# First doubling of the triangular inverses: sixteen 128x128 problems against one compact tile on the array's four diagonal 32x32 corners

## The chip, the cores and the metric

One core of one Trainium2 chip. The metric is the device time of one execution in microseconds, median of the runs of the same kernel on the same chip. The names used below: TensorE (PE, its weight load is PEld), VectorE (DVE), ScalarE (ACT), GpSimd (POOL) and SyncE (SP), which issues the DMAs.

## What is computed

One residual block with 512 tokens and 1024 features in float32: a SwiGLU FFN, a token mixer, a second FFN. The mixer has two groups of heads, a multi-head latent attention and a gated delta rule. The change touches the delta rule alone, which solves for every head (4) and every chunk of 64 tokens (8 of them) a unit lower triangular system:

```python
decay = jnp.exp(jnp.where(incl, G[..., :, None] - G[..., None, :], -jnp.inf))
kk = jnp.einsum('bhncd,bhnsd->bhncs', k, k)
A = jnp.where(strict, beta[..., :, None] * kk * decay, 0.0)
M = A + jnp.eye(CHUNK, dtype=A.dtype)
rhs = jnp.concatenate([v * beta[..., None], k * (beta * jnp.exp(G))[..., None]], axis=-1)
W = lax.linalg.triangular_solve(M, rhs, left_side=True, lower=True, unit_diagonal=True)
u, wk = W[..., :GDN_DV], W[..., GDN_DV:]
```

The kernel works with blocks of 128 tokens in place of 64 (the recurrence allows any chunk), so it needs sixteen inverses of 128x128: four blocks p times four heads h.

## The kernel before, in words

The kernel runs FFN 1, the mixer and FFN 2 one after the other; nearly all of TensorE's work is dense products with weights, each made of three products of rounded halves (lines 475 to 477 and 360). Within the mixer the small work is written as Python generators. A step of such a generator emits a few instructions and yields. `dense_units` (line 1469) emits two k-tiles of a weight product, that is six matmuls of 512 columns, and then steps the sides: `chain` (delta rule), `deltas` (its other operands) and `att` (attention). The framework then orders each engine's instructions by its own estimate of when they are ready, except where the code ties one instruction behind another (`follow`, line 149); so the order on TensorE is near to the order of emission, not equal to it.

The chain of the delta rule is: `delta_k`, `delta_a` (the matrix A of every head, transposed, as tile `at`, one per head, with the four blocks p side by side), then `bases()` (line 2264), then `solving` (products with the inverses, lines 1923 and 1932) and the recurrence over the blocks (`recur`, lines 1958 to 1985).

`bases()` builds the sixteen inverses by doubling. `base_blocks` inverts the 16x16 diagonal blocks row by row on VectorE and brings them through DRAM into the tile `t16`: 128 rows, and per problem q = 4p + h 16 columns. Then `inverse(p)` makes, for one block p, the inverses of the 32x32 diagonal blocks of all four heads: it spreads `t16` into a block-diagonal tile `t` of 128 x (4 heads x 128) with the mask `dmask` (line 1808), turns each 32x32 square of it (`flip`, line 1804) into `u`, multiplies with A (line 1814), masks the product with `lmask` into `Y` (line 1816), multiplies again (line 1820), subtracts (line 1822) and turns the result (line 1804 again). The four generators `inverse(0)` to `inverse(3)` stand in one `Side` of width 4 and are stepped in turn: three steps each, twelve in all, of which the last of each emits nothing. `inverse_levels` does the next two doublings, 32 to 64 (lines 1852 to 1868) and 64 to 128 (lines 1880 to 1901); the first of them already uses 32x32 matmuls at two places of the array, rows 0 and columns 32, rows 64 and columns 96, and packs its results 32 columns per problem.

The masks are made once, during FFN 1 (`masks`, line 1367), on GpSimd.

Of the kernel before, what the change touches and what calls it, by code (L numbers as in the profile page):

```python
# [16 lines left out]
ALU = mybir.AluOpType  # L17
AX = mybir.AxisListType

P = 128  # L20
# [3 lines left out]
NB = NT // P  # L24
# [75 lines left out]
class Block:  # L100
# [1266 lines left out]
    def masks(self):  # L1367
        nc = self.nc
        tile = self.slot(s="mk")
        room = iter([tile[:, i * P:(i + 1) * P] for i in range(4)])  # L1370
        g = nc.gpsimd
        half = next(room).bitcast(BF16)
        self.eye, self.emask = half[:, :P], half[:, P:]
        nc.vector.tensor_copy(self.eye, self.ident)
        g.memset(self.emask, 0.0)
        g.affine_select(out=self.emask, in_=self.emask, pattern=[[1, P]], compare_op=ALU.is_ge, fill=-1.0e30, base=0,
                        channel_multiplier=-1)
        self.triu = next(room)
        g.affine_select(out=self.triu, in_=self.ones, pattern=[[1, P]], compare_op=ALU.is_ge, fill=0.0, base=0,
                        channel_multiplier=-1)  # L1380
        self.dmask = next(room)
        dv = self.dmask.rearrange("p (j i) -> p j i", i=16)
        g.affine_select(out=dv, in_=self.ones.rearrange("p (j i) -> p j i", i=16), pattern=[[-16, 8], [0, 16]],
                        compare_op=ALU.is_ge, fill=0.0, base=0, channel_multiplier=1)
        g.affine_select(out=dv, in_=dv, pattern=[[16, 8], [0, 16]], compare_op=ALU.is_ge, fill=0.0, base=15,
                        channel_multiplier=-1)
        self.lmask = next(room)
        mv = self.lmask.rearrange("p (j i) -> p j i", i=16)
        g.affine_select(out=mv, in_=self.ones.rearrange("p (j i) -> p j i", i=16), pattern=[[-16, 8], [0, 16]],
                        compare_op=ALU.is_ge, fill=0.0, base=-16, channel_multiplier=1)  # L1390
        g.affine_select(out=mv, in_=mv, pattern=[[16, 8], [0, 16]], compare_op=ALU.is_ge, fill=0.0, base=31,
                        channel_multiplier=-1)
        g.memset(mv[:, 1:8:2, :], 0.0)

        am = self.const([P, 192], BF16, s="am")
        g.memset(am, 0.0)
        g.memset(am[0:1, 0:64], 1.0)
        g.memset(am[0:1, 128:192], -1.0e30)
        self.amask = am[:, :P], am[:, P:]
        sel = self.slot(F32R, s="sel")  # L1400
        g.memset(sel.bitcast(F32), 0.0)
        self.sel = sel.rearrange("p (h c) -> p h c", h=4)
        for o in (0, 32):
            nc.vector.tensor_copy(self.sel[o:o + 4], self.ident[o:o + 4, o:o + 4].unsqueeze(2).to_broadcast([4, 4, P]))
# [386 lines left out]
        yield  # L1791
        yield

    def inverse(self, p):

        nc = self.nc
        h4 = lambda x: x.rearrange("p (h d) -> p h d", h=4)
        hs = lambda h: slice(h * P, (h + 1) * P)
        at = lambda h, rows=slice(0, P), c0=0, c1=P: self.at[h][rows, p * P + c0:p * P + c1]

        def flip(src):

            t = self.slot(s="T")
            nc.vector.transpose(out=t, in_=src)
            return t

        t = self.slot(s="t0")
        self.mul(t.rearrange("p (h i c) -> p h i c", h=4, i=8),
                 self.t16[:, 4 * p:4 * p + 4, :].unsqueeze(2).to_broadcast([P, 4, 8, 16]),
                 self.dmask.rearrange("p (i c) -> p i c", i=8).unsqueeze(1).to_broadcast([P, 4, 8, 16]))  # L1810
        u = flip(t)
        py = self.aux()
        for h in range(4):
            nc.tensor.matmul(py[:, hs(h)], at(h), t[:, hs(h)], start=True, stop=True)
        y = self.slot(s="Y")
        self.mul(h4(y), h4(py), self.lmask.unsqueeze(1).to_broadcast([P, 4, P]))
        yield
        pz = self.aux()
        for h in range(4):
            nc.tensor.matmul(pz[:, hs(h)], y[:, hs(h)], u[:, hs(h)], start=True, stop=True)  # L1820
        un = self.slot(s="U")
        nc.vector.tensor_tensor(out=un, in0=u, in1=pz, op=ALU.subtract)
        t = flip(un)
        yield

        self.un[p], self.tn[p] = un, t

    def inverse_levels(self):

        nc = self.nc  # L1830
        h4 = lambda x: x.rearrange("p (h d) -> p h d", h=4)
        at = lambda p, h, rows, c0, c1: self.at[h][rows, p * P + c0:p * P + c1]
        un, each = self.un, [(p, h) for p in reversed(range(NB)) for h in range(4)]
        sides = [(j, slice(j, j + 32), slice(j + 32, j + 64)) for j in (0, 64)]

        @contextmanager
        def together():
            with self.traced() as block:
                yield
            after = None  # L1840
            for i in block:
                if i.engine == mybir.EngineType.PE:
                    if after:
                        self.follow(i, after)
                    after = i.name

        py, y = self.aux(), self.slot(s="Y")
        with together():
            for p, h in each:
                c = P * p + 32 * h  # L1850
                for j, a, b in sides:
                    nc.tensor.matmul(py[b, c:c + 32], at(p, h, a, j + 32, j + 64),
                                     self.tn[p][a, h * P + j:h * P + j + 32], start=True, stop=True,
                                     tile_position=(j, j + 32))
        nc.scalar.copy(y[sides[0][2], :], py[sides[0][2], :])
        nc.vector.tensor_copy(y[sides[1][2], :], py[sides[1][2], :])
        yield
        yield
        pz = self.aux()
        with together():  # L1860
            for p, h in each:
                c = P * p + 32 * h
                for j, a, b in sides:
                    nc.tensor.matmul(pz[a, c:c + 32], y[b, c:c + 32], un[p][b, h * P + j + 32:h * P + j + 64],
                                     start=True, stop=True, tile_position=(j + 32, j))
        for p in reversed(range(NB)):
            for j, a, b in sides:
                nc.vector.tensor_scalar(out=h4(un[p][a, :])[:, :, j + 32:j + 64],
                                        in0=pz[a, P * p:P * p + P].rearrange("p (h c) -> p h c", h=4), scalar1=-1.0,
# [3 lines left out]
        a, b = slice(0, 64), slice(64, P)  # L1873
# [1 line left out]
        at64 = lambda p, h: slice(256 * (p % 2) + 64 * h, 256 * (p % 2) + 64 * h + 64)  # L1875
        pts, ts, ys = [self.aux() for _ in pairs], [self.slot(s="T") for _ in pairs], [self.slot(s="Y") for _ in pairs]
        both = [(n, p, h) for n, ps in enumerate(pairs) for p in reversed(ps) for h in range(4)]
        with together():
            for n, p, h in both:
                nc.tensor.transpose(pts[n][a, at64(p, h)], un[p][a, h * P:h * P + 64], self.ident[a, a])  # L1880
        for t, pt in zip(ts, pts):
# [1 line left out]
        yield  # L1883
        yield
        pys = [self.aux() for _ in pairs]
        with together():
            for n, p, h in both:
                nc.tensor.matmul(pys[n][b, at64(p, h)], at(p, h, a, 64, P), ts[n][a, at64(p, h)], start=True, stop=True,
                                 tile_position=(0, 64))
# [2 lines left out]
        yield  # L1892
        yield
        pzs = [self.aux() for _ in pairs]
        with together():
            for n, p, h in both:
                nc.tensor.matmul(pzs[n][a, at64(p, h)], ys[n][b, at64(p, h)], un[p][b, h * P + 64:h * P + P], start=True,
                                 stop=True, tile_position=(64, 0))
        for n, ps in reversed(list(enumerate(pairs))):
            for p in ps:  # L1900
                nc.vector.tensor_scalar(out=h4(un[p][a, :])[:, :, 64:],
                                        in0=pzs[n][a, 256 * (p % 2):256 * (p % 2) + 256].rearrange("p (h c) -> p h c", h=4),
# [314 lines left out]
    def mixer(self, norms):  # L2217
        nc, tc = self.nc, self.tc
# [19 lines left out]
            for t in tiles:  # L2238
                self.table(t, t, AF.Silu, after=after)

        self.inv, self.un, self.tn = ([None] * NB for _ in range(3))
        self.kd, self.us, self.o, self.wk, self.vb, self.kbg = ([None] * NB for _ in range(6))
        self.S = None

# [18 lines left out]

        def bases():
            yield from self.base_blocks()
            inv = Side(wide=4)
            inv.add(*(self.inverse(p) for p in range(NB)))
            while inv.open or inv.todo:
                inv.step()
                yield  # L2270
            yield from self.inverse_levels()

        chain.add(self.delta_k(kT), self.delta_a(kT), bases())
        self.dense_units(4, Rates(sides, (1, 0, 1.5)), 1, conv_done(0, qT))
        silu(qT)
# [23 lines left out]
        fill = Side()  # L2299
# [203 lines left out]
```

## Time and profile before

| | before |
|---|---|
| median of 3 runs | 1021.51 us (1021.45 to 1022.29) |
| profiled execution, own time | 1021.74 us |
| its span | 1020.0 us |
| outside the span | 1.74 us |
| TensorE busy | 1010.3 us (99%) |
| VectorE busy | 809.1 us (79%) |
| ScalarE busy | 513.5 us (50%) |
| GpSimd busy | 28.9 us (3%) |

How to read it: the span is the time from the first to the last instruction of one execution. Matmuls are pipelined, so a busy time of TensorE adds records that overlap; what a batch of matmuls costs on the path is read from the chain of waits, which gives every piece the time from the end of the piece before it to its own end. A float32 matmul (as opposed to the rounded halves) stands in the trace as two records, each with a weight load of its own. A row "x8" is eight such records merged.

### The profile page before, as it was taken

How to read it: one execution, taken by the hardware profiler on the slowest of the kernel's cores; microseconds unless marked ns; L12 is line 12 of the kernel's file. 1: busy time of each engine (PE TensorE's matmuls, PEld its weight loads, DVE VectorE, ACT ScalarE, POOL GpSimd, SP SyncE). 2: the span in 40 equal slices, each digit the busy share in tenths (PEclk: the TensorE clock that was granted, in tenths of full speed). 3: DMA queues.
4: the chain of work that ended last, by engine and by line, in shares of the span. 5: the costliest groups of instructions: out<-in, count | busy, mean ns of one | idle time of the engine just before them, and what ended most of it. 6: DMA issues, size and time to landing. Idle time of an engine off the chain costs nothing.

```text
span 1020.0 us, 17205 instructions
## 1 busy us (share of the span) xinstructions
PE 1010.3 (99%) x6729; PEld 908.1 (89%) x6729; DVE 809.1 (79%) x1428; ACT 513.5 (50%) x921; POOL 28.9 (3%) x74
## 2 busy tenths in 40 slices
PE   7999999999999999999999999999999999999998
PEld 6788899999887899888888888998999999987988
DVE  4789788887787847878988658777888888789995
ACT  4453455556422225558846465464555555634443
POOL 0000000000200000100000011000000000000000
PEclk9999999999999999999999999999999999999999
DMA  9998233333688835321222210213233333372612
GB/s 326 291 280 263 63 104 108 100 115 110 187 295 292 284 74 173 82 62 42 67 73 52 70 36 21 84 49 96 85 102 106 107 102 110 113 253 72 175 42 63
DMA packets 203775, 130.79 MB, mean 128 GB/s; under 512 B 14241, under 2 KB 188334, under 8 KB 203694
## 3 DMA queue, kind: packets, MB, share of 16 engines
q1 hardware_dynamic: 203694, 129.70, 42.1%
q8 instruction: 53, 0.87, 0.3%
q14 instruction: 28, 0.23, 0.1%
HBM read 127.18 MB, written 2.49 MB: 127 GB/s over the span
## 4 chain that ended last, share of the span: by engine, by line
PE 95%; DVE 3%; DMA 1%; issue 0%; ACT 0%; SPq 0%; POOL 0%; DVEq 0%
PE pa L360 17%; PE pa L475 16%; PE pa L476 15%; PE pa L477 15%; PE pb L360 13%; PE pa L1228 3%; PE pb L1228 2%; PE pb L2186 1%; PE pb L2166 1%; PE pb L475 1%; PE pb L476 1%; PE pb L477 1%; PE pb L1735 1%; PE pb L673 1%; DMA vecs<-in_b_ada 1%; DVE cv L1679 1%
## 5 line engine op out<-in xcount | busy, mean ns | idle before, releaser
L275 DVE TENSOR_TENSOR wl<-wr,wh 128x1024 fp32r<-128x1024 f32 x105 | 128.2, 1222 | 45.1 <-ACT wh L279 45.0
L234 ACT CAST wh<-wr 128x1024 fp32r<-128x1024 f32 (+1 forms) x87 | 87.3, 1012 | 146.5 <-PE pa L476 121.3
L475 PE MATMUL pa<-hh,wh 128*128 128x512 f32 (+1 forms) x357 | 137.2, 384 | 0.0
L477 PE MATMUL pa<-hh,wl 128*128 128x512 f32 (+1 forms) x357 | 134.9, 378 | 0.0
L476 PE MATMUL pa<-hl,wh 128*128 128x512 f32 (+1 forms) x357 | 134.7, 377 | 0.0
L235 DVE TENSOR_TENSOR wl<-wr,wh 128x1024 fp32r<-128x1024 f32 (+1 forms) x87 | 101.5, 1172 | 41.3 <-ACT wh L234 41.1
L279 ACT CAST wh<-wr 128x1024 fp32r<-128x1024 f32 x105 | 107.4, 1052 | 13.0 <-DVE wr L275 7.2
L475 PE MATMUL pa<-ah,wh 128*128 128x512 f32 (+1 forms) x294 | 110.5, 376 | 0.0
L476 PE MATMUL pa<-al,wh 128*128 128x512 f32 (+1 forms) x294 | 110.1, 374 | 0.0
L477 PE MATMUL pa<-ah,wl 128*128 128x512 f32 (+1 forms) x294 | 109.7, 373 | 0.0
L475 PEld LDWEIGHTS pa<-hh,wh 128*128 128x128 f32 x357 | 67.3, 189 | 13.1 <-issue 1.6
L844 DVE SCALAR_TENSOR_TENSOR aa<-ar,sc,aa 128x512 f32<-128x512 f32 x98 | 73.5, 750 | 6.8 <-DMA ar<-in_w_ada 4.9
L477 PEld LDWEIGHTS pa<-hh,wl 128*128 128x128 f32 x357 | 67.2, 188 | 12.0
L476 PEld LDWEIGHTS pa<-hl,wh 128*128 128x128 f32 x357 | 67.3, 189 | 10.7
L275 DVE TENSOR_TENSOR wr<-wr,wr 128x512 f32<-128x512 f32 x105 | 72.5, 690 | 2.0
L360 PE MATMUL pa<-hh,wh 128*128 128x256 f32 x240 | 68.0, 283 | 0.0
L360 PE MATMUL pa<-th,wh 128*128 128x256 f32 x240 | 67.9, 283 | 0.0
L360 PE MATMUL pa<-tl,wh 128*128 128x256 f32 x240 | 67.9, 283 | 0.0
L360 PE MATMUL pa<-th,wl 128*128 128x256 f32 x240 | 67.9, 283 | 0.0
L360 PE MATMUL pa<-hl,wh 128*128 128x256 f32 x240 | 67.9, 283 | 0.0
L360 PE MATMUL pa<-hh,wl 128*128 128x256 f32 x240 | 67.9, 283 | 0.0
L475 PEld LDWEIGHTS pa<-ah,wh 128*128 128x128 f32 x294 | 55.3, 188 | 12.2 <-ACT wh L234 2.5
(485 smaller groups left out, 2619.1 us busy)
## 6 DMA issues: line engine op xcount, KB each, us to landing
wr<-in_ffn_w_in SPq DMA_DIRECT2D x79, 512.0 KB
ar<-in_w_ada SPq DMA_DIRECT2D x96, 256.0 KB
wr<-in_ffn_w_out SPq DMA_DIRECT2D x32, 512.0 KB
ar<-in_w_ada SPq DMA_DIRECT2D x22, 512.0 KB
wr<-in_w_in SPq DMA_DIRECT2D x21, 512.0 KB
wr<-in_ffn_w_out SPq DMA_DIRECT2D x16, 384.0 KB
wr<-in_w_out SPq DMA_DIRECT2D x8, 512.0 KB
wr<-in_ffn_w_in SPq DMA_DIRECT2D x8, 384.0 KB
```

The source lines that it names most:

```text
L234: self.nc.scalar.copy(hi, raw)
L235: self.nc.vector.tensor_tensor(out=lo, in0=raw, in1=hi.bitcast(F32), op=ALU.subtract)
L275: sub = lambda out, x, y: nc.vector.tensor_tensor(out=out, in0=x, in1=y, op=ALU.subtract)
L279: nc.scalar.copy(hi[:, :n], raw[:, :n])
L360: nc.tensor.matmul(z, a[:, j, :], b, start=start and j == 0 and i == 0, stop=j == 3 and i == 2, skip_group_check=not start)
L475: mm(out, wh, xh, start=start, stop=False)
L476: mm(out, wh, xl, start=False, stop=False)
L477: mm(out, wl, xh, start=False, stop=stop)
L673: nc.tensor.matmul(pg[32 * q:32 * q + 32, :256], self.sc[:, kc:kc + 1].to_broadcast([P, 32]), a[kc], start=(e == 0), stop=(e == 1), tile_p ...
L844: nc.vector.scalar_tensor_tensor(out=acc, in0=a, scalar=sc, in1=acc, op0=ALU.mult, op1=ALU.add)
L1228: nc.tensor.matmul(z, a[:, j, :], b, start=start and j == 0 and i == 0, stop=j == 3 and i == 2, skip_group_check=not start)
L1679: nc.vector.scalar_tensor_tensor(out=a[:, d:], in0=p[:, :NT - d], scalar=wj(3 - d), in1=a[:, d:], op0=ALU.mult, op1=ALU.add)
```

## The change

The first doubling is done once, for all sixteen problems, in one tile of 128 x (16 problems x 32 columns) in place of four tiles of 128 x (4 heads x 128). For each problem q and each diagonal 32x32 block j there is one 32x32 matmul at `tile_position=(32j, 32j)`, that is 64 matmuls in each of the two products, tied in order by `together` (now a method). The mask of `t16` has two columns (`halves`), `lmask` 32. The 32x32 inverses stay packed as `u32` and `t32`, which `inverse_levels` reads directly; four VectorE or GpSimd multiplications with `quads` spread `u32` into the four block-diagonal tiles `un[p]`. `inverse` is one generator with five yields.

```diff
         self.triu = next(room)
...
-        self.dmask = next(room)
...
+        room = next(room)
+        by16, self.halves, self.quads, self.lmask = room[:, :8], room[:, 8:10], room[:, 12:16], room[:, 32:64]
+        g.affine_select(out=by16, in_=self.ones[:, :8], pattern=[[-16, 8]], compare_op=ALU.is_ge, fill=0.0, base=0,
+                        channel_multiplier=1)
+        g.affine_select(out=by16, in_=by16, pattern=[[16, 8]], compare_op=ALU.is_ge, fill=0.0, base=15,
                         channel_multiplier=-1)
...
+        nc.vector.tensor_reduce(out=self.halves, in_=by16.rearrange("p (j e) -> p e j", e=2), axis=AX.X, op=ALU.add)
+        nc.vector.tensor_reduce(out=self.quads, in_=by16.rearrange("p (j e) -> p j e", e=2), axis=AX.X, op=ALU.add)
+        g.memset(self.lmask[:, 16:], 0.0)
+        nc.vector.tensor_copy(self.lmask[:, :16], self.halves[:, 1:2].to_broadcast([P, 16]))
...
-    def inverse(self, p):
+    def inverse(self):
...
+        q32 = lambda x: x.rearrange("p (q c) -> p q c", q=16)
+        spots = [(q, j, slice(32 * j, 32 * j + 32), slice(32 * q, 32 * q + 32)) for q in reversed(range(16))
+                 for j in range(4)]
...
         t = self.slot(s="t0")
-        self.mul(t.rearrange("p (h i c) -> p h i c", h=4, i=8),
-                 self.t16[:, 4 * p:4 * p + 4, :].unsqueeze(2).to_broadcast([P, 4, 8, 16]),
-                 self.dmask.rearrange("p (i c) -> p i c", i=8).unsqueeze(1).to_broadcast([P, 4, 8, 16]))
+        self.mul(t.rearrange("p (q e c) -> p q e c", q=16, e=2),
+                 self.t16.unsqueeze(2).to_broadcast([P, 16, 2, 16]),
+                 self.halves.unsqueeze(1).unsqueeze(3).to_broadcast([P, 16, 2, 16]))
         u = flip(t)
+        yield
         py = self.aux()
-        for h in range(4):
-            nc.tensor.matmul(py[:, hs(h)], at(h), t[:, hs(h)], start=True, stop=True)
+        with self.together():
+            for q, j, rows, cols in spots:
+                c = P * (q // 4) + 32 * j
+                nc.tensor.matmul(py[rows, cols], self.at[q % 4][rows, c:c + 32], t[rows, cols], start=True, stop=True,
+                                 tile_position=(32 * j, 32 * j))
         y = self.slot(s="Y")
-        self.mul(h4(y), h4(py), self.lmask.unsqueeze(1).to_broadcast([P, 4, P]))
+        self.mul(q32(y), q32(py), self.lmask.unsqueeze(1).to_broadcast([P, 16, 32]))
+        yield
         yield
         pz = self.aux()
-        for h in range(4):
-            nc.tensor.matmul(pz[:, hs(h)], y[:, hs(h)], u[:, hs(h)], start=True, stop=True)
-        un = self.slot(s="U")
-        nc.vector.tensor_tensor(out=un, in0=u, in1=pz, op=ALU.subtract)
-        t = flip(un)
-        yield
-
-        self.un[p], self.tn[p] = un, t
+        with self.together():
+            for q, j, rows, cols in spots:
+                nc.tensor.matmul(pz[rows, cols], y[rows, cols], u[rows, cols], start=True, stop=True,
+                                 tile_position=(32 * j, 32 * j))
+        self.u32 = self.slot(s="U")
+        nc.vector.tensor_tensor(out=self.u32, in0=u, in1=pz, op=ALU.subtract)
+        self.t32 = flip(self.u32)
+        yield
+        for p in reversed(range(NB)):
+            self.un[p] = self.slot(s="U")
+            self.mul(self.un[p].rearrange("p (h j c) -> p h j c", h=4, j=4),
+                     q32(self.u32)[:, 4 * p:4 * p + 4].unsqueeze(2).to_broadcast([P, 4, 4, 32]),
+                     self.quads.unsqueeze(1).unsqueeze(3).to_broadcast([P, 4, 4, 32]), nc.gpsimd if p % 2 else None)
+        yield
...
-                                     self.tn[p][a, h * P + j:h * P + j + 32], start=True, stop=True,
+                                     self.t32[a, c:c + 32], start=True, stop=True,
...
-                    nc.tensor.matmul(pz[a, c:c + 32], y[b, c:c + 32], un[p][b, h * P + j + 32:h * P + j + 64],
+                    nc.tensor.matmul(pz[a, c:c + 32], y[b, c:c + 32], self.u32[b, c:c + 32],
...
         def bases():
             yield from self.base_blocks()
-            inv = Side(wide=4)
-            inv.add(*(self.inverse(p) for p in range(NB)))
-            while inv.open or inv.todo:
-                inv.step()
-                yield
+            yield from self.inverse()
             yield from self.inverse_levels()
```

## Rows read from the trace of the kernel before

**Rows 1.** The page's first part: busy time, share of the span, instructions.

```profile
PE 1010.3 (99%) x6729; PEld 908.1 (89%) x6729; DVE 809.1 (79%) x1428; ACT 513.5 (50%) x921; POOL 28.9 (3%) x74
```

**Rows 2.** Waits between engines, whole span, TensorE: total us, times, longest.

```profile
PE pb L526 <- DMA xt<-in_x: 4.7, 1, 4.7
PE pb L541 <- DMA vecs<-in_b_ada: 0.5, 1, 0.5
PE pb L2039 <- DVE qrT L2099: 0.4, 1, 0.4
```

**Rows 3.** Busy time by stretch: stretch, length, PE, PEld, DVE, ACT, POOL, clock, DMA.

```profile
541.00:556.00 15.00, 14.92 (x92) 12.32 (x91) 13.05 (x24) 8.83 (x15) 1.01 (x1) 1.00 0.17 57
556.00:564.00 8.00, 8.00 (x71) 7.86 (x71) 7.03 (x15) 2.98 (x9) 0.00 (x0) 1.00 0.01 2
...
600.00:625.00 25.00, 24.91 (x186) 23.23 (x185) 16.51 (x34) 15.81 (x35) 5.04 (x5) 1.00 0.01 2
```

**Rows 4.** Chain of waits, 540 to 600 us: start us, us on the path, what.

```profile
541.27 1.10 PE pb L1814 x8
...
546.24 0.89 PE pb L1814 x8
...
550.43 0.89 PE pb L1814 x8
...
554.46 1.13 PE pb L1814 x8
556.03 0.97 PE pb L1820 x8
...
558.11 0.89 PE pb L1820 x8
...
559.72 0.97 PE pb L1820 x8
...
562.13 0.89 PE pb L1820 x8
...
564.60 0.44 PE pb L1687 x4
...
576.66 1.13 PE pb L1852 x64
577.79 0.58 PE pb L2208 x4
...
582.01 1.13 PE pb L1864 x64
...
590.63 2.00 PE pb L1888 x32
```

**Rows 5.** VectorE by line, 535 to 601 us: busy us, mean ns, idle before.

```profile
L1804 DVE STREAM_TRANSPOSE T<-U 128x512 f32<-128x512 f32 x4 | 2.8, 708 | 0.1
L1804 DVE STREAM_TRANSPOSE T<-t 128x512 f32<-128x512 f32 x4 | 2.8, 708 | 0.0
L1467 DVE TENSOR_TENSOR t<-t,mk 128x512 f32<-128x512 f32 x4 | 2.7, 686 | 0.5 <-DMA t<-t_d 0.5
L1822 DVE TENSOR_TENSOR U<-T,pb 128x512 f32<-128x512 f32 x4 | 2.7, 684 | 0.8 <-PE pb L1820 0.8
L1467 DVE TENSOR_TENSOR Y<-pb,mk 128x512 f32<-128x512 f32 x4 | 2.7, 682 | 1.1 <-PE pb L1814 1.1
```

**Rows 6.** GpSimd in order of time: start us, us, line, operation, idle before.

```profile
254.34 5.00 POOL L1379 TENSOR_SCALAR_AFFINE_SELECT mk<-ones 128x128 f32<-128x128 f32 x1
...
611.12 1.04 POOL L1467 TENSOR_TENSOR Sg<-S,gl 128x512 f32<-128x512 f32 x1
```

**Rows 7.** Waits between engines, 535 to 660 us: total us, times, longest.

```profile
ACT wh L234 <- PE pa L476: 14.3, 5, 6.4
```

**Rows 8.** VectorE in order of time, 575 to 600 us: one attention block.

```profile
590.67 0.69 DVE L2171 TENSOR_REDUCE mx<-pb 128x1 f32<-128x512 f32 x1 [0.57 <-PE pb L2169]
591.39 0.16 DVE L2173 TENSOR_TENSOR mx<-mx,rqn 128x1 f32<-128x1 f32 x1
592.55 0.16 DVE L2198 SCALAR_TENSOR_TENSOR ve<-al 128x4 f32<-128x4 f32 x1 [1.00 <-ACT pr L207]
```

More of the change, by code (lines that the diff above doesn't have):

```diff
@@ L1380, in masks @@
                         channel_multiplier=-1)
-        self.dmask = next(room)
[L1382 to L1385, printed above, removed]
-                        channel_multiplier=-1)
[L1387 to L1393, printed above, removed]
+        room = next(room)
[3 more added lines that the diff above has]
+        g.affine_select(out=by16, in_=by16, pattern=[[16, 8]], compare_op=ALU.is_ge, fill=0.0, base=15,
+                        channel_multiplier=-1)
+        nc.vector.tensor_reduce(out=self.halves, in_=by16.rearrange("p (j e) -> p e j", e=2), axis=AX.X, op=ALU.add)
+        nc.vector.tensor_reduce(out=self.quads, in_=by16.rearrange("p (j e) -> p j e", e=2), axis=AX.X, op=ALU.add)
+        g.memset(self.lmask[:, 16:], 0.0)
+        nc.vector.tensor_copy(self.lmask[:, :16], self.halves[:, 1:2].to_broadcast([P, 16]))
         am = self.const([P, 192], BF16, s="am")
@@ L1792, in base_blocks, with together @@
         yield
-    def inverse(self, p):
+    @contextmanager
+    def together(self):
+        with self.traced() as block:
+            yield
+        after = None
+        for i in block:
+            if i.engine == mybir.EngineType.PE:
+                if after:
+                    self.follow(i, after)
+                after = i.name
+    def inverse(self):
         nc = self.nc
-        h4 = lambda x: x.rearrange("p (h d) -> p h d", h=4)
-        hs = lambda h: slice(h * P, (h + 1) * P)
-        at = lambda h, rows=slice(0, P), c0=0, c1=P: self.at[h][rows, p * P + c0:p * P + c1]
+        q32 = lambda x: x.rearrange("p (q c) -> p q c", q=16)
+        spots = [(q, j, slice(32 * j, 32 * j + 32), slice(32 * q, 32 * q + 32)) for q in reversed(range(16))
+                 for j in range(4)]
         def flip(src):
@@ L1834, in inverse_levels @@
         sides = [(j, slice(j, j + 32), slice(j + 32, j + 64)) for j in (0, 64)]
-        @contextmanager
-        def together():
-            with self.traced() as block:
-                yield
[L1840 to L1845, printed above, removed]
         py, y = self.aux(), self.slot(s="Y")
-        with together():
+        with self.together():
             for p, h in each:
@@ L1859, in inverse_levels @@
         pz = self.aux()
-        with together():
+        with self.together():
             for p, h in each:
@@ L1877, in inverse_levels @@
         both = [(n, p, h) for n, ps in enumerate(pairs) for p in reversed(ps) for h in range(4)]
-        with together():
+        with self.together():
             for n, p, h in both:
@@ L1885, in inverse_levels @@
         pys = [self.aux() for _ in pairs]
-        with together():
+        with self.together():
             for n, p, h in both:
@@ L1894, in inverse_levels @@
         pzs = [self.aux() for _ in pairs]
-        with together():
+        with self.together():
             for n, p, h in both:
@@ L2239, in silu @@
                 self.table(t, t, AF.Silu, after=after)
-        self.inv, self.un, self.tn = ([None] * NB for _ in range(3))
+        self.inv, self.un = ([None] * NB for _ in range(2))
         self.kd, self.us, self.o, self.wk, self.vb, self.kbg = ([None] * NB for _ in range(6))
```

## The prediction

> **What bounds the kernel now.** I read the busy times first: TensorE works 1010.3 of 1020.0 us, VectorE 809.1, ScalarE 513.5, so the first suspect is TensorE [rows 1]. Busy time alone is weak evidence, because records of matmuls overlap; the waits settle it. Over the whole span TensorE waited for another engine or a DMA for 4.7 us at the very start (the input x) and then for 0.5 and 0.4 us; no other wait of its matmuls is listed [rows 2]. The rest is TensorE's own work, back to back. So the rule for this kernel: a microsecond of work taken off TensorE's queue is a microsecond off the end, as long as something else is ready to take its place, and a microsecond taken off VectorE is worth nothing in itself.
>
> Then I looked at the stretches in which the first doubling runs. From 541 to 556 us TensorE is busy for 14.92 of 15.00 us, from 556 to 564 us for all 8.00; VectorE is nearly as full there, 13.05 of 15.00 and 7.03 of 8.00 [rows 3]. So the stretch is bound by TensorE with VectorE close behind: what is taken off both of them helps doubly, in that the second doesn't become the bound.
>
> Last the chain of waits, which gives the price of a batch on the path. The first doubling is eight batches of 128x128 float32 matmuls, four at line 1814 and four at line 1820. All eight are on the chain [rows 4].
>
> **What is removed on TensorE.** The eight batches take 1.10 + 0.89 + 0.89 + 1.13 us (line 1814) and 0.97 + 0.89 + 0.97 + 0.89 us (line 1820), together 7.73 us [rows 4]. 0.89 us for eight records is 111 ns a record; what is above that in five of the eight is restart after other work.
>
> **What is added on TensorE.** Two batches of 64 matmuls. A float32 matmul is two records (the 32 matmuls of line 1852 are "x64"), so a batch is 128 records of 32x32, 32 for each of the four corners. The nearest rows are the batches of lines 1852 and 1864, the same 32x32 shape at two places of the array: 64 records in 1.13 us each [rows 4]. That is 32 records per place in 1.13 us, 35 ns a record.
>
> Do these two places work side by side or in turn? The trace answers through the widths. A record of 128 columns takes 111 ns; one of 64 columns at one place (line 1888, 32 records in 2.00 us) takes 62.5 ns [rows 4]. Half the width saved 49 ns, so half again should save some 24 ns: about 38 ns for a record of 32 columns at one place, an estimate from these two rows. The batch of line 1852 started a record every 1.13/64 = 17.7 ns, about half of that. So two places ran fully side by side; the time of a batch is set by the number of records per place, which is 32 there and 32 here.
>
> Bounds for the new batch. If four corners also run side by side: 1.13 us, as at line 1852. If no more than two do, or if the queue can't start a record more often than every 17.7 ns: 128 x 17.7 ns = 2.26 us. If the corners take turns: 128 x 35 ns = 4.52 us. I take 1.3 us, close to the low end, since line 1852 has the same count per place; the 0.17 us on top are my allowance for four starts in place of two within the same 35 ns, of which no row tells.
>
> A batch of another shape also costs its surroundings something. Behind line 1852 the four records of line 2208 took 0.58 us, where the same shape behind matmuls of its own kind, at line 1687, took 0.44 us: 0.14 us for the way back [rows 4]. The way in is contained in the 1.13 us. So one new batch is 1.3 + 0.14 = 1.44 us and both are 2.88 us. TensorE's path loses 7.73 - 2.88 = **4.85 us**.
>
> **What changes on VectorE and GpSimd.** Before, five operations for each of four blocks: spread 0.686, two turns of 0.708, `Y` 0.682, subtraction 0.684, 3.47 us a block, 13.9 us in all [rows 5]. After: the same five once (all still 512 columns wide), 3.47 us, and two of the four spreads of `u32`, at the price of the spread before, 0.69 each: 4.85 us. VectorE loses 9.0 us in the stretch where it is fullest. I cost that at nothing, since TensorE never waited long for it there; it is what keeps VectorE from getting in the way. The other two spreads go to GpSimd. The nearest row is `Sg`, the same size with a broadcast operand: 1.04 us [rows 6], so 2.1 us for both. Their results are first needed where line 1868 writes into `un[p]`, behind the batches of lines 1852 and 1864; between them and the spreads lie a yield, a batch, two more yields and a batch. In the trace of before 1852 started at 576.66 and 1864 ended at 583.14 us: 6.5 us of cover [rows 4]. If the cover were gone, the price is the 2.1 us on VectorE's queue, and from there on the next doubling (transposes of line 1880). Whether GpSimd slows VectorE beside it, this trace doesn't show, as VectorE was idle during `Sg`; even at double time for 2.1 us VectorE keeps 6.9 of its 9 us.
>
> **The new waits.** The product of line 1814's successor now has a yield between the spread and the matmuls, where before it came at once (that is why the first batch took 1.10). `Y` and the second product have two yields between them, before one. One step of the chain was 3.9 us long there: the first batch of line 1814 ended at 542.37, the second, a step later, began at 546.24 us [rows 4]. Against that stand 0.68 us for `Y` and a queue on VectorE. I cost both waits at nothing. Behind such a wait on TensorE is queued everything, the dense products too; if VectorE has two or three operations of 0.7 us ahead [rows 5] and the step is as short as the 2 us between the batches of line 1820 [rows 4], each wait may cost 0.5 to 1 us. That end goes into the range.
>
> **Masks.** Three affine selects of 128x128 fewer on GpSimd, three tiny operations more on VectorE, during FFN 1. The first select of that group took 5.00 us at 254.34 us [rows 6], so VectorE could wait some microseconds if it came to the reductions at once. TensorE has no wait in that stage [rows 2], and the weights are split ahead of it. Nothing, with an end of 1 us.
>
> **What moves.** The twelve steps of the chain become five, so everything behind (both later doublings, the solves, the recurrence) is emitted seven steps earlier, against the same dense products. The work of TensorE is the same; its cover is distributed otherwise. In the recurrence after it, 600 to 625 us, TensorE was busy for 24.91 of 25.00 us [rows 3]: there is hardly anything to be gained, and something to lose. I take zero, with 2 us to both sides in the forecast's own range.
>
> **Sum.** Span 1020.0 - 4.85 = 1015.15 us. The profiled execution took 1.74 us more than its span, which gives 1016.9, and the median of the runs lies 0.23 us below it: **1016.7 us**.
>
> **The rivals.** *Only two corners at a time.* Each batch 2.26 + 0.14 us, both 4.80, gain 2.93 us: 1018.6 us. For it: no row has more than two 32x32 places. Against it: in line 1852 the two places did not slow each other at all. Chance 0.17.
>
> *The corners take turns.* All four write into the same bank of PSUM, in different partitions. If that serialises them, a batch is 4.52 + 0.14 us, both 9.32, 1.59 us more than before: 1023.1 us, within the bound of no change. Against it: the two places of line 1852 also wrote into one tile `pb`, from two groups of rows, and kept 17.7 ns a record [rows 4]. Chance 0.07. The Trainium skill, "TensorEngine Tiling (Array Packing)", section "Restrictions and Gotchas", has this as a rule: different row tiles can't access the same PSUM bank at once and should write to different banks. By that rule line 1852 would have taken turns too; the trace disagrees for two row groups, and for four no row here shows it.
>
> *The gain is given back in part.* The change takes the work away but TensorE finds nothing ready in its place, because the dense products wait for their weights' halves: 1018 to 1021.5 us. Against it: ScalarE waited 14.3 us for TensorE's matmuls before it could split the next weights [rows 7], so weights wait for TensorE and not the other way round. Chance 0.10.
>
> *Slower: the attention's last blocks lie bare.* The while loop behind the dense stage ends when the solves are done. Seven steps earlier means three or four turns fewer, and the attention steps that those turns took along (four each) are drained in one go before the recurrence goes on, without the chain's batches between them. A block's way from the scores through VectorE's maximum and ScalarE's exponential lasted from 590.67, when VectorE began on the scores, to 592.55 us, when the first reader of the exponential's sums began: 1.9 us [rows 8]. Each one that lies bare costs TensorE 1.9 us; at three the gain is gone, at four (7.6 us) the kernel stands at 1016.7 + 7.6 = 1024.3 us. It decides from the fourth. Against it: four blocks are open at once and cover each other, and products of the output matrix are ready to be pulled forward. Chance 0.08.
>
> **How the numbers follow.** Forecast 0.58, own range 1014.0 to 1018.5; the rivals 0.17, 0.07, 0.10 and 0.08. Faster by over 0.2% (2.04 us, about what a measurement of this kernel can tell from no change) means below 1019.5 us: the forecast, two corners at a time but for its upper edge, and some of the third rival, 0.75. Within 0.2%: corners in turn, the rest of the third and that edge, 0.17. Slower: the fourth, 0.08. The range reaches from 1014.0 over the second case and most of the third to 1020.5; the turns, the bare blocks and the last third of the third rival are outside, 0.19.
>
> **What would show it.** Each step in the profile after: two batches x128 on the chain with 1.1 to 1.5 us each (2.3: second case; 4.5: turns); lines 1804, 1808, 1816 and 1822 on VectorE once in place of four times; two spreads on GpSimd near 1.0 us with nobody waiting; line 1852 some 15 us earlier; TensorE's list of waits no longer than before. The prediction is wrong if TensorE has new waits for `Y`, for `pT` or for weights between 541 and 640 us that add up to more than 2 us, or if a later stage gives the time back.

## The result and the profile after

The changed kernel takes 1024.7 us (median of 12 runs, 1023.35 to 1026.06), the kernel before 1021.38 us beside it (12 runs, 1020.82 to 1023.49). The ratio is 1.003, with a 95% interval of 1.0022 to 1.0038: **slower by 3.3 us**, where 4.8 us faster was forecast. The profiled execution of after took 1024.43 us itself, its span is 1022.7 us, 2.7 us longer than before's.

First the busy times of after (share of the span, instructions), to set against [rows 1].

```profile
PE 1008.7 (99%) x6921; PEld 905.2 (89%) x6921; DVE 802.4 (78%) x1418; ACT 512.8 (50%) x921; POOL 30.7 (3%) x74
```

Each of the two busy engines has less to do, TensorE by 1.6 us and VectorE by 6.7 us, and the kernel is longer all the same. So the time is not in work but in waits, or in work done at another speed. The list of TensorE's waits over the whole span (for what it waited: total us, times, longest us) answers to [rows 2]:

```profile
PE pb L526 <- DMA xt<-in_x: 4.8, 1, 4.8
PE pb L2217 <- DVE on L1464: 4.3, 1, 4.3
PE pa L477 <- DVE wl L235: 0.6, 1, 0.6
...
```

Two waits are new: 4.3 us at line 2217 (2208 in before) and 0.6 us at line 477. Neither is at a line that the change rewrites. The stretches of [rows 3], in after (stretch, length, PE, PEld, DVE, ACT, POOL, granted clock, DMA), then the two that lie around the new wait:

```profile
541.00:556.00 15.00, 15.00 (x385) 12.39 (x382) 12.57 (x22) 10.77 (x21) 3.46 (x3) 1.00 0.05 17
600.00:625.00 25.00, 20.70 (x134) 19.06 (x133) 14.40 (x29) 13.73 (x31) 5.24 (x5) 0.86 0.07 22
```

```profile
604.00:609.10 5.10, 0.80 (x8) 0.59 (x8) 3.85 (x7) 1.55 (x4) 1.93 (x2) 0.82 0.34 103
607.50:614.40 6.90, 5.36 (x23) 5.18 (x24) 2.73 (x4) 4.20 (x7) 2.66 (x3) 0.52 0.09 30
```

Where the change is, TensorE is as full as before. Sixty microseconds later it works 20.70 of 25.00 us, where it worked 24.91 before. From 604 to 609.1 us it does nearly nothing, and for the 6.9 us from 607.5 on the granted clock is 0.52: half of 2.4 GHz, that is 1.2 GHz. The chain of waits (start us, us on the path, what) shows both ends of the story, the part of [rows 4] that was changed and the place of the new wait:

```profile
540.95 1.22 PE pb L1826 x82
...
546.37 1.22 PE pb L1835 x82
...
552.19 1.13 PE pb L1861 x64
...
587.77 1.78 PE pb L1932 x16
...
599.35 0.89 PE pb L1932 x8
...
602.97 0.95 ACT wh L234
...
603.95 1.23 DVE wl L235
605.17 0.59 DVE gs L2005
605.76 0.59 DVE as L2035
606.36 0.66 DVE ml L2223
...
607.17 1.01 POOL ry L220
...
608.21 0.70 DVE on L1464
...
609.04 1.09 PE pb L2217 x4
610.13 1.71 PE pb L1967 x8
611.84 1.71 PE pb L1975 x8
```

The upper three lines are the forecast come true: the two new batches cost 1.22 us each in place of eight batches with 7.73 us (the chain lists 82 of the 128 records of each), and line 1861 (line 1852 before) comes at 552.19 us, 24.5 us earlier than in [rows 4], where the prediction looked for some 15. Below, TensorE drops out of the chain at 601 us, and VectorE, ScalarE and GpSimd stand in it until 609 us. It is the end of the attention's last head (`attended()`): square (`hn`) and sum (`as`) of the head's output, a power on GpSimd (`ry`), the scaling on VectorE (`on`), the four transposes of line 2217. Behind the wait eight records of the recurrence take 1.71 us instead of the 0.89 us that the same shape takes at 599.35.

The same place in before, TensorE's instructions in order of time (start us, us, line, operation, records):

```profile
599.32 1.83 PE L2186 MATMUL pb<-vn,pT 128*128 128x128 f32 x14
...
601.42 1.95 PE L1923 MATMUL pb<-vb,U 128*128 128x128 f32 x16
...
608.82 0.63 PE L2208 MATMUL pb<-ident,on 128*128 128x128 f32 x4
```

Between the last values of the attention (line 2186) and the last transposes (line 2208) TensorE had the batches of the solves and the recurrence's first two (lines 1973 and 1981) to do, from 601.42 to 608.8 us: 7.4 us of cover for the head's end. The text calls them all the solves. In after the same (lines 1932, 1941, 1982, 1990) began at 587.77 us and were over at 601.15 us. The attention's last values come behind them, and the last copy of the head's output, on ScalarE, is the row from which the head's end runs:

```profile
602.48 1.83 PE L2195 MATMUL pb<-vn,pT 128*128 128x128 f32 x14
...
604.34 0.27 ACT L2196 COPY ao<-pb 128x128 f32<-128x128 f32 x1 [0.26 <-PE pb L2195]
```

From 604.61 us, where that copy ends, to the transposes at 609.04 us TensorE has next to nothing to lie over the 4.4 us. Not all of the 4.4 us are the head's own. ScalarE began the square, `hn`, at 604.64 us and needed 0.63 us, but VectorE came to its sum `as` only behind `gs`, which ended at 605.76, and did 0.66 us of `ml`, for the head before, ahead of the rest. These two are some 1.2 us; about 3.2 us are the way itself.

So the theory that the experiments test: **the change gains what was forecast, but the twelve steps of the chain that became five bring the solves seven steps earlier, and away from the one place in which TensorE needed them.** Rivals: the compact tile itself disturbs the later stage (a spread on GpSimd, a buffer); or something earlier than the solves (the spreads or the later doublings) is the cover; or the halved clock, not the wait, is what costs.

### The profile page after: what moved, and what is told of

Read it like the earlier page. It is cut to its first block, busy times and chain, and to the rows that moved or that the text cites. A ratio compares the mean times of both kernels' runs of the same rounds, so it can differ in the third digit from the quotient of the medians.

```text
span 1022.7 us, 17568 instructions
## 1 busy us (share of the span) xinstructions
PE 1008.7 (99%) x6921; PEld 905.2 (89%) x6921; DVE 802.4 (78%) x1418; ACT 512.8 (50%) x921; POOL 30.7 (3%) x74
## 4 chain that ended last, share of the span: by engine, by line
PE 93%; DVE 4%; ACT 1%; SPq 1%; issue 1%; DMA 1%; POOL 0%; DVEq 0%; ACTq 0%
PE pa L360 17%; PE pa L475 15%; PE pa L476 15%; PE pa L477 15%; PE pb L360 13%; PE pa L1228 3%; PE pb L1228 2%; PE pb L2175 1%; PE pb L475 1%; PE pb L477 1%; PE pb L476 1%; PE pb L2195 1%; PE pb L1732 1%; SPq L139 1%; DVE wl L235 1%
```

## The experiments

All are the changed kernel with the edit shown (`pad7_dve` with that of `pad7` besides), but for `before_short`, which is the kernel before with one edit. No kernel leaves work out; `busy` adds work.

### pad7: the seven steps given back

```diff
             yield from self.inverse()
+            for _ in range(7):
+                yield
             yield from self.inverse_levels()
```

> The changed kernel with seven empty steps of the chain between the compact doubling and the later doublings, so that these, the solves and the recurrence are emitted at the step at which they were before. Theory 1 (the cover moved: the solves no longer stand beside the attention's last head, TensorE waits 4.3 us there, and its clock then falls for 6.8 us): the wait of TensorE for the last head's scaled output is gone, the granted clock stays at 1.00, and what the compact batches save is left, about 5 us: 1015.5 to 1018.0 us. Rival (the compact tile costs it itself: packed matmuls, spreads on GpSimd, waits for Y): the wait moves or stays and the time is 1022 to 1026 us.

Measured: 1017.64 us (4 runs, 1016.27 to 1018.39) against 1021.56; ratio 0.9959 (0.9945 to 0.9974). Seven steps that do nothing are worth 7 us to the changed kernel. The wait at line 2217 is gone. From the first batch of line 2195 (2186 in before) with ten records to the last of line 2016 (2007), the chain has 540.20 to 637.47 = 97.27 us; in before the same two stand at 538.65 and 640.77, 102.12 us. The stretch is shorter by 4.85 us, the forecast's sum; in `pad7_dve`, below, it is 97.27 us again. What lies over the head's end now is shown by the second profile of this kernel, `pad7_again`: TensorE in order of time, the first and the last of the solves' batches and the transposes behind them.

```profile
596.70 1.95 PE L1932 MATMUL pb<-vb,U 128*128 128x128 f32 x16
...
602.95 1.06 PE L1932 MATMUL pb<-vb,U 128*128 128x128 f32 x8
604.10 0.63 PE L2217 MATMUL pb<-ident,on 128*128 128x128 f32 x4
```

### solve_late: the same steps just ahead of the solves

```diff
             yield from self.inverse_levels()
+            for _ in range(7):
+                yield
```

> The changed kernel with the seven empty steps behind the later doublings instead, so that only the solves and the recurrence come at their old step. Theory 1 in its narrow form (it is the solves, seven batches of 0.89 us in the kernel before, that covered the attention's last head): as with the steps ahead of the later doublings, 1015.5 to 1018.5 us with no wait of TensorE above 1 us around 600 us. If it is the later doublings' batches that were the cover: 1021 to 1025 us.

Measured: 1018.04 us (5 runs, 1017.6 to 1018.86); ratio 0.9964 (0.9951 to 0.9977). Here the later doublings stay early and only what follows them is late, and the time is that of `pad7`. So it is the solves (with the recurrence's first two batches among them) that were the cover, not the spreads or the doublings.

### before_short: the kernel before with a short chain

```diff
-                inv.step()
+                inv.step(2)
```

> The kernel before with two steps of the inverses in one step of the chain, so that twelve steps become six and everything behind comes six steps earlier, with the 128x128 products as they were. Theory 1: the attention's last head lies bare here too, TensorE waits 3 to 5 us and the clock falls behind it: 1025 to 1029 us. Rival (the compact tile is the cause): within 1 us of the kernel before, 1020.5 to 1022.5 us.

Measured: 1028.69 us (4 runs, 1027.73 to 1029.0); ratio 1.0066 (1.0049 to 1.0083). Its list of TensorE's waits and its chain:

```profile
PE pb L2208 <- DVE on L1467: 3.9, 1, 3.9
PE pa L477 <- DVE wl L235: 0.6, 1, 0.6
```

```profile
612.64 1.09 PE pb L2208 x4
613.73 1.71 PE pb L1958 x8
...
```

The old arithmetic, taken in six steps rather than twelve, has both new waits of after and the slow records behind the first, and loses 7.1 us: 3.9 and 0.6 us of waiting and some 2.7 us of slow records. The compact tile is not the cause; the number of steps is.

### busy: TensorE kept at work during the wait

The four transposes' tile is written four times with the head's output first; the transposes overwrite it, so the result is the same and TensorE has work before the wait ends.

```diff
         pt = self.aux()
+        if h == 3:
+            for _ in range(4):
+                nc.tensor.matmul(pt, self.ident, self.ao[h], start=True, stop=True)
```

> The changed kernel with four idle-time matmuls (128x128 by 512 columns, float32, some 3.5 us, results overwritten by what follows) on TensorE's queue ahead of the last head's transposes, in the place where it waited 4.3 us. Theory 1 splits the 7 us lost there in two: the wait itself, 4.3 us, which this leaves as it is, and the half clock that follows it, about 2.7 us (6.8 us at half speed, of which 1.5 us lie within the wait). If the clock falls because TensorE stands still, it stays at 1.00 here and the kernel takes 1021.5 to 1022.5 us. If the slow batches behind the wait have another cause (memory, weights), they stay at 1.7 us and the kernel at 1024 to 1026 us.

Measured: 1022.7 us (10 runs, 1022.24 to 1024.39) against 1021.54 (25 runs); ratio 1.0016 (1.0006 to 1.0025). It is 1.2 us slower than before, where after is 3.3 us slower, and 2.0 us below after's median; the range expected for a clock that stays up ended 0.2 us lower. TensorE in order of time, then the stretch that had the half clock:

```profile
604.72 3.70 PE L2218 MATMUL pb<-ao,ident 128*128 128x512 f32 x8
609.02 0.66 PE L2220 MATMUL pb<-ident,on 128*128 128x128 f32 x4 [0.60 <-DVE on L1464]
609.51 1.06 PE L1967 MATMUL pb<-S,w 128*128 128x128 f32 x8
```

```profile
607.50:614.40 6.90, 6.30 (x42) 5.09 (x41) 2.64 (x4) 4.66 (x9) 2.72 (x3) 1.00 0.08 27
```

With other work before them the transposes still begin at 609.02 us, since `on` comes no earlier; but the clock stays at 1.00 and line 1967 has its old speed (1.06 us in this view, 1.91 us in the same view of after). So the loss has two parts, the wait and the clock behind it. In after's chain the slow records cost 0.65 (line 2217, 1.09 against 0.44 us) + 0.82 + 0.82 (lines 1967 and 1975, 1.71 against 0.89 us) + some 0.3 us of two dense records, 2.6 us. `busy` got some 2.0 of it back; of the rest, 0.3 us is a new wait at line 475, for `xT`, at 621 us.

### pad3 and pad11: is seven a special number?

As `pad7`, with `range(3)` and `range(11)`.

> Three empty steps in place of seven. If the loss depends on how much of the solves is left when the attention's last head ends, TensorE's wait there shrinks with each turn of the loop that comes later: between 0 and 4 us of wait, 1017 to 1023 us. If it is one event that is there or not, 1017 to 1018.5 us or 1024 to 1025 us.

Measured: 1020.93 us (10 runs, 1019.84 to 1022.4); ratio 0.9995 (0.9986 to 1.0004), no difference from before.

> Eleven empty steps: later than in the kernel before. If the cover is complete with seven steps, nothing more is gained, 1016.5 to 1018.5 us, and the solves may now come behind the attention's end and lengthen the way to the recurrence: up to 1021 us. If the schedule of before was itself not yet the best, below 1016.5 us.

Measured: 1021.1 us (10 runs, 1020.25 to 1022.54); ratio 0.9997 (0.9988 to 1.0007), no difference either. TensorE in order of time in `pad3`, then its wait in `pad11`:

```profile
599.89 1.73 PE L2195 MATMUL pb<-vn,pT 128*128 128x128 f32 x14
...
603.74 0.40 PE L477 MATMUL pa<-mh,wl 128*128 128x512 f32 x1
605.98 0.81 PE L2217 MATMUL pb<-ident,on 128*128 128x128 f32 x4 [1.85 <-DVE on L1464]
```

```profile
PE pb L2217 <- DVE on L1464: 2.2, 1, 2.2
```

With three steps the wait is down from 4.3 to 1.9 us, but not by part of the solves: those in front of the attention's last values end at 600.05 us, as these begin. What lies over the head's end is nine dense products, from 601.81 to 604.14 us, 2.3 us of cover. So the wait is what is left of the head's way when the work that happens to stand behind it, of whatever kind, is done. With eleven steps the wait comes back from the other side, as the chain of `pad11` shows:

```profile
597.19 0.75 DVE U L1910 x2
...
598.67 0.66 DVE U L1910 x2
599.33 0.61 DVE on L1464
...
600.07 1.08 PE pb L2217 x4
601.16 3.41 PE pb L1932 x16
```

The last doubling now stands beside the head's end, its copies (`U`, line 1910) are ahead of `on` in VectorE's queue, and the solves, which wait for `U`, come behind the transposes instead of beside them. The clock is at half there again: line 1932 takes 3.41 us for sixteen records, where the profile of `pad7_again` has 1.79 us. Of the four numbers of steps that were run (0, 3, 7, 11), seven is the best; those between weren't tried.

### corners and pairs: what makes the corners run side by side

The same 128 records in another order: corner after corner, then two corners in turn and after them the other two.

```diff
-        spots = [(q, j, ...) for q in reversed(range(16))
-                 for j in range(4)]
+        spots = [(q, j, ...) for j in range(4)
+                 for q in reversed(range(16))]
```

```diff
+        spots = [(q, j, ...) for k in (0, 2)
+                 for q in reversed(range(16)) for j in (k, k + 1)]
```

> The changed kernel with the 64 matmuls of each compact batch issued corner after corner in place of one problem's four corners in turn. If the corners overlap because neighbours in the queue go to different corners, a batch rises from 1.22 us to about 4.5 us (128 records of 35 ns) and the kernel by 6 to 7 us. If the array keeps the corners apart whatever the order, a batch stays at 1.2 to 1.3 us.

> The changed kernel with each compact batch issued for two corners alternately, then for the other two. By the rule that neighbours in the queue overlap when they go to different corners and a corner takes 35 ns a record, a batch takes 2.2 to 2.3 us. If four neighbours overlap in another way than by corner (any four records in flight), it stays near 1.2 us.

Measured, one execution each and so without an interval: 1032.69 and 1026.15 us. Both keep the wait of 4.3 us; what counts here is the batches on the chain, `corners` first:

```profile
540.95 4.62 PE pb L1826 x128
...
552.17 3.86 PE pb L1835 x128
```

```profile
547.25 2.05 PE pb L1835 x126
```

One corner at a time costs 3.86 us (30 ns a record) at full clock, two 2.05 us, four 1.22 us; the first two are a little less than was expected (4.5 and 2.2 to 2.3). So the corners do work side by side in the changed kernel, and the order in the queue is what decides it. They do so nearly in full, not quite: a record and corner takes 30 ns alone, 32 with one neighbour (2.05 us for 64) and 38 with three (1.22 us for 32). The first batch of `corners` is longer because the clock fell in it (below, with the hardware).

### pad7_again and pad7_dve: the better version

`pad7` once more, and with all four spreads on VectorE:

```diff
-                     ...to_broadcast([P, 4, 4, 32]), nc.gpsimd if p % 2 else None)
+                     ...to_broadcast([P, 4, 4, 32]))
```

> The kernel with seven empty steps once more, for a closer interval: by theory 1 the prediction's own sum (4.85 us off TensorE's path) is what is left when the cover stands where it was, so 1016.2 to 1018.0 us against 1021.5 us. If more than 1 us of the sum is lost for another reason, 1018.0 to 1020 us.

> The same with all four spreads of the 32x32 inverses on VectorE in place of two on GpSimd. By the prediction's step (the spreads are covered on either engine, 6.5 us of cover for 2.1 us) no change against the kernel with seven empty steps, within 0.7 us. If GpSimd's spreads had held up VectorE or the next doubling, 0.5 to 2 us less.

Measured: 1016.94 us (5 runs, 1016.04 to 1017.8), ratio 0.9955 (0.9942 to 0.9969), and 1016.97 us (4 runs, 1015.93 to 1018.1), ratio 0.9955 (0.9941 to 0.9968), against 1021.49 us. **The changed kernel with seven empty steps beats both kernels, by 4.55 us and 7.8 us.** Where the spreads run is worth nothing. The waits of `pad7_again`:

```profile
PE pb L526 <- DMA xt<-in_x: 4.6, 1, 4.6
...
PE pb L1826 <- DVE t L1464: 0.3, 1, 0.3
```

From 600 to 625 us its TensorE is busy for 24.91 of 25.00 us at a granted clock of 1.00.

**The account.** From the span of `pad7_again`, 1015.2 us, to that of after, 1022.7 us, it is 7.5 us: the wait of 4.3, the slow records 2.6, the wait of 0.6 us at line 477. From before to `pad7_again` it is -4.8 us. Together: 1020.0 - 4.8 + 7.5 = 1022.7 us. The same reckoning for `pad3`, with 1.9 us of waiting, 0.6 us at line 477 and some 1.8 us of slow records, gives 1020.0 - 4.8 + 4.3 = 1019.5 us; its span was 1019.4. Why the 0.6 us at line 477 comes with too short a chain was not taken apart. Nor is the account of whole spans good to better than about a microsecond: `pad7` in its two profiles had spans of 1016.7 and 1015.2 us. That difference lies ahead of the changed part: in the first profile TensorE waited 1.1 us at line 541 and twice 0.4 us at line 673 before that part began, and in the second not at all there.

## Why the prediction was wrong

**What bounds the kernel: right.** TensorE's own queue bounds it, and what was taken from that queue came off the end as soon as the cover was back. VectorE's 6.7 us less bought nothing that shows: the stretch in `pad7` is shorter by TensorE's sum alone.

**The batches: right.** 1.22 us each against 1.3 assumed: the four corners run side by side, nearly in full. The stretch with everything in it lost 4.85 us in `pad7`, and the forecast had 4.85. That the two agree to the hundredth is partly luck. The batches alone saved 7.73 - 2.44 = 5.29 us, so 0.44 us went elsewhere, where the allowance for the way back was 0.28; it can't be seen apart. A small slip on the way: four of the eight old batches, not five, lie above 0.89 us [rows 4]; the sum of 7.73 us is right.

**The rivals of the corners: refuted.** Two at a time (2.26 us, measured 2.05 where the order forces it) and in turns (4.52, measured 3.86) are what the batches cost when the corners are queued that way, not what the change does. The rule of the Trainium skill weighed ahead of it ("TensorEngine Tiling (Array Packing)", "Restrictions and Gotchas": no two row tiles at one PSUM bank at the same time) doesn't show here for four row groups either: all four wrote one tile `pb`, at 1.22 us for 128 records. The Trainium skill's "TensorE: Matmul & The Clock Gate", "Part 3: Packing small matmuls — row/col tiling", says that matmuls keep the order of the program and that a weight load overlaps them only where its row group differs; with that the 1.22, 2.05 and 3.86 us for four, two and one corner agree.

**GpSimd and VectorE: right in effect, wrong in size.** The spreads on GpSimd took 1.04 and 1.49 us, and VectorE beside them waited some 1.7 us (below). VectorE lost 6.7 us and not 9.0, close to the 6.9 that the prediction gave for the case that GpSimd slows it. No TensorE instruction waited for either.

**The new waits and the masks: right at nothing.** No wait of a TensorE instruction at lines 1826, 1835 or 1861 stands in after's list. In `pad7_again` there is one, of 0.3 us.

**What moves: the step that failed.** "I take zero, with 2 us to both sides" was argued from the recurrence's stretch, 24.91 of 25.00 us busy [rows 3]: hardly anything to gain there, something to lose. The text saw the loss as possible and priced it only in a rival, by other work. A stage that is full shows how well its waits are covered, and says nothing of what covers them. What should have been read is the order of TensorE's instructions from 601 to 609 us, shown above: an operation whose input comes by ScalarE, VectorE, GpSimd and VectorE again, with 7.4 us of the moved stage before it. That way takes 4.4 us in after, from the end of ScalarE's last copy of the head's output at 604.61 us to 609.04. So moving the solves seven steps takes the cover away, and the price is a wait of 4.3 us, with the clock on top. `pad3` shows that this was not bound to happen in full: there nine dense products came behind the last values and left 1.9 us of it.

**The rival on the slower side had the place and not the mechanism.** "The attention's last blocks lie bare" gave 1024.3 us and a chance of 0.08; that 1024.7 us was measured is luck. It priced softmax blocks at 1.9 us each [rows 8] and let the fourth decide. What lay bare was one thing, the end of the last head, once; and it was dearer than its idle time, since the clock halved behind it. The wait alone, with 4.3 us, eats nearly all of the gain; 2.6 and 0.6 us more turn it into a loss. The chance was too low for a step of which the text itself said that the cover "is distributed otherwise".

## What to carry to other kernels

When an edit shortens a chain of steps that is interleaved with others, it also moves everything behind the chain; follow each moved stage to its old place and ask which waiting operation it stood in front of, and how long that operation's way over the other engines is. Price a bared way at its whole length, with what stands ahead of it in the other engines' queues and less the work that still lies over it, and add the matmuls that follow it at half clock. If the local gain shows in the trace and the end is later, put the old number of steps back with empty ones before giving the change up: here that alone made 3.3 us slower into 4.55 us faster.

## What the runs showed of the hardware

**A busy TensorE can lose its clock.** In `corners` the granted clock fell although TensorE was listed as busy without a gap (stretch, length, PE, PEld, DVE, ACT, POOL, granted clock, DMA):

```profile
541.00:546.00 5.00, 5.00 (x129) 4.94 (x130) 3.45 (x6) 3.67 (x7) 0.00 (x0) 0.77 0.08 28
546.00:551.00 5.00, 5.00 (x18) 3.40 (x18) 1.16 (x3) 0.67 (x2) 0.00 (x0) 0.55 0.02 3
```

What TensorE did before was 4.62 us of 32x32 products at one corner at a time; the clock fell while it ran, and the attention's products behind it went at 1.2 GHz until 550.5 us. The second such batch, from 552.17 us, ran its 3.86 us at full clock, so the batch alone doesn't decide it, and the cause is not shown. In after, the same products at four corners kept the clock at 1.00 (the stretch from 541 to 556 us above). In after the fall came behind 4.3 us of waiting; in `pad3` 1.9 us of waiting was followed by half clock for 3.4 us, and in `pad11` the clock fell within a wait of 2.2 us and stayed at half for some 6.9 us, from 599 us on. So the length of the wait alone doesn't give the price.

**GpSimd and VectorE keep each other waiting.** In after the two spreads on GpSimd lie beside multiplications on VectorE, both engines in order of time (start us, us, line, operation):

```profile
550.80 1.04 POOL L1464 TENSOR_TENSOR U<-U,mk 128x512 f32<-128x512 f32 x1
551.80 1.49 POOL L1464 TENSOR_TENSOR U<-U,mk 128x512 f32<-128x512 f32 x1
```

```profile
550.87 1.52 DVE L1464 TENSOR_TENSOR on<-ao,ry 128x512 f32<-128x512 f32 x1
552.32 2.12 DVE L1464 TENSOR_TENSOR U<-U,mk 128x512 f32<-128x512 f32 x2
```

The 2.12 us are a spread of 1.52 and one of 0.68 us. Alone, `on` takes 0.70 us (at 608.21 in after's chain), a spread on VectorE 0.69 [rows 5], and a multiplication of this size on GpSimd 1.04 (`Sg`, [rows 6]). The first spread on GpSimd keeps its 1.04 us with `on` beside it, and from there the ends alternate: GpSimd 551.84, VectorE 552.39, GpSimd 553.29, VectorE 553.84. So these rows read as turns, a whole operation at a time, and not as both engines running slower; the last spread on VectorE, with GpSimd done, has its 0.68 us. In `pad7_dve`, with GpSimd idle, all four spreads on VectorE take this long together:

```profile
551.94 2.49 DVE L1464 TENSOR_TENSOR U<-U,mk 128x512 f32<-128x512 f32 x4
```

With `on` (0.69 us there) VectorE is done with them in 3.1 us, where with two of the four on GpSimd it took 3.6 us, from 550.87 to 554.44. GpSimd's help cost VectorE half a microsecond.
